# Counting two microseconds more, in the kernel's own scheduler, until a transfer of rotated heads has landed

## The chip, the cores and the metric

The kernel runs on one core of one Trainium2 chip. Five engines of that core matter here: TensorE (PE in the profile, with its weight loads as PEld), VectorE (DVE), ScalarE (ACT), GpSimd (POOL) and SyncE (SP), whose queue issues every DMA of this kernel. The metric is device time in microseconds; lower is better. "Before" is a median of three runs, and one further execution was taken by the hardware profiler, which gives the span (first to last instruction) and all rows quoted below.

## The reference

A decoder trunk with 256 tokens of width 1024 and two layers, all in float32. The first layer is causal multi-head latent attention (MLA), the second is MoBA block-sparse attention over keys and values computed once from the stream after the first layer. With 256 tokens there is a single MoBA block, so the second layer is in effect causal attention with 16 heads of 64. Each layer ends in a gated output projection, a residual and a LayerNorm.

```python
def moba_shared_kv(x, w_kv, cos, sin):
    kv = x @ w_kv
    k = kv[..., :WIDTH_B].reshape(B, S, H_B, HD_B)
    v = kv[..., WIDTH_B:].reshape(B, S, H_B, HD_B)
    k = apply_rope(k, ...)

def moba_mixer(x, k_blocks, v_blocks, k_mean, w_in, w_o, cos, sin):
    h = x @ w_in
    q, gate = h[..., :WIDTH_B], h[..., WIDTH_B:]
    q = apply_rope(q.reshape(B, S, H_B, HD_B), ...)
    ...                                   # scores, causal mask, softmax, values
    return (o * jax.nn.silu(gate)) @ w_o

def reference(x, ...):
    for layer in range(DEPTH):
        ...
        x = layer_norm(ALPHA * x + y, ln_g[layer], ln_b[layer])
    return x
```

## The kernel before, in words

**Arithmetic.** Every float32 weight and activation is split into a rounded part and a remainder (the tiles `wh` and `wl`, `act_h` and `act_l`, `big_h` and `big_l`; ACT casts, DVE or POOL subtracts). A product is then three matmuls: high by high, low by high, high by low. Two groups of products matter below. A *chunk* is a product of 128 output features by 256 tokens over 8 slices of the inner dimension, 24 matmuls of 256 columns into a PSUM bank called `proj`. A *token product* has 128 tokens as output partitions and 512 (or 258, or 256) features as columns.

**Stages.** First the MLA layer; its output projection (`oa`), LayerNorm, and the value projection of the second layer (`vb`). Then the stage that the change touches, the MoBA attention, from about 160 us on. It has 24 chunks: eight of queries (`qb`), eight of keys (`kb`), eight of gates (`gb`). Then the output projection (`ob`), whose result is kept for token half 0 in two `proj` banks and for token half 1 in two `s` banks and one `proj` bank, followed by the last LayerNorm.

**Rotated heads and their transfers.** `rope_moba` makes one chunk of queries and one of keys in a bank, multiplies by cosine and sine (DVE), adds halves (POOL or DVE) and splits the result into the tile `R` (named `x_h`). The heads' rows then have to change partitions: `move_heads` does this with eight DMAs for each pair of heads, four of 96 KB and four of 64 KB, from `R` into one of three tiles `HT` (`kq0`, `kq1`, `x_l`), so that rows `kq<-x_h` and `x_l<-x_h` in the profile are these transfers. The scores of a pair of heads (`s<-kq` or `s<-x_l`, three matmuls a head) need all eight. After the scores come, for each head: mask and exponent (tile `e`; DVE and ACT), three transposes on PE (`pt<-ident,e`), a copy by ACT, and for every two pairs the products with the values (`pv<-pt,V`), which DVE multiplies by the gates into `oa` and ACT, POOL and DVE split into `big_h` and `big_l`, the left operand of the output projection.

**What sets the order.** Nothing is issued in the order of the source. Every operation is recorded with an estimated duration, and `Schedule.order` replays the program on paper: for each engine it keeps what is ready, and puts down next the operation that can start first, with priorities from the longest way to the end and the place in the source. Each engine then executes its list strictly in the written order; waits are semaphores. A transfer ends on paper at its queue start, plus its size, plus 1300 ns, plus a constant that its caller may give:

```python
x = max(t + 1100, dma)
dma = x + o.size / 330.0
o.end = dma + 1300 + o.late
lanes.append(o.end + 100)
```

`late` is 2000 for seven of the eight first loads of inputs and weights (`LATE`) and zero for everything else. `lanes` holds the paper's ends of transfers; with `LANES` (8) of them open, the next transfer waits on paper.

**The end of the program.** `token_products("ob", ...)` goes over the eight slices of the inner dimension, token half 1 lagging by eight. Slices 6 and 7 of the weights lie in the tiles `x_h` and `x_l`, so rows `proj<-x_h,big_h` and `proj<-x_l,big_h` are the last slices of token half 0, and `s<-x_h,big_h` those of token half 1. When token half 0 is complete, `finish_b` runs `layer_norm` on DVE in pieces of 512 columns (residual, statistics, two passes with gain and bias; rows with tile `m`, `bst`, `mv`). `last_b` does the same for token half 1 in pieces (0 to 512, 512 to 768, 768 to 1024): rows `m<-m,s`, `bst<-m`, `ms`, `act_h<-m,ms,lng`, and last `act_h<-act_h,mv,lnb`, after each of which but the first a store to the output is issued.

Of the kernel before, what the change touches and what calls it, by code (L numbers as in the profile page):

```python
# [53 lines left out]
PLAIN = 2  # L54
PIECES = 4
LATE = 2000

LANES = 8

# [79 lines left out]
def A(x):  # L139
    if isinstance(x, View):  # L140
        return x.ap()
    return x.tile() if isinstance(x, Val) else x
# [225 lines left out]
def trunk(ctx, tc, W0, xtok, W, WO, gq, gkv, lng, lnb, cosa, sina, coska, sinka, cosb, sinb, maskd, identd, out):  # L368
# [22 lines left out]
    def dma(o, i, size, part=False, r=None, late=0):  # L391
        sc.op("sp", 650 if part else 525, lambda: nc.sync.dma_start(A(o), A(i)), [i] if r is None else r, [o], size).late = late
# [55 lines left out]
    def split(h, l, src, n, scale=None, eng="dve"):  # L448
        if scale is None:
            act(h, src, n)  # L450
            tt(l, src, h.f32(), ALU.subtract, n, eng)
        else:
            act(h, src, n, AF.Identity, scale=scale)
            stt(l, src, scale, h.f32(), ALU.mult, ALU.subtract, n)
# [10 lines left out]
    def load_raw():  # L465
# [3 lines left out]
        if u < 8:  # L469

            for c0, c1 in ((0, 512), (512, 1280)) if u < PLAIN else ((0, 1280),):
                dma(r[:, c0:c1].at(c0), W0[u, :, c0:c1], (c1 - c0) * 512, late=LATE * (u > 0))
            split(xh[:, u, :].at(u), xl[:, u, :].at(u), r[:, 0:S].at(0), S)
# [128 lines left out]
    for k in range(8):  # L602
        w = weights("g1", k)
        a, b = xs(k)
        for c in range(8):
            o = g1[c // 2][:, (c % 2) * S:(c % 2) * S + S]
            if k < PLAIN and c < 2:
                u, v = first_raws[k][:, S + c * P:S + (c + 1) * P].at(0), first_raws[k][:, 0:S].at(0)
# [323 lines left out]
    def move_heads(step):  # L932
        while moves and moves[0][0] - 3 <= step:
            p, R, base = moves.pop(0)
            hd = HT[p % 3]
            for s in range(2):
                r0 = base + 32 * s
                for v in range(2):
                    dma(hd[32 * v:32 * v + 32, s, 0:3, :].at((s, v, 0)).f32(), R[r0:r0 + 32, v, 1:4, :].at(None).f32(), 98304, True)
                    dma(hd[64 + 32 * v:96 + 32 * v, s, 0:2, :].at((s, v, 1)).f32(), R[r0:r0 + 32, v, 0:4:2, :].at(None).f32(), 65536, True)  # L940

    def heads_moba(p):
        hd = HT[p % 3]
# [6 lines left out]
    def fill_b(step):  # L950
        for nm, i in PLAN_B[step + 1]:
            if nm == "r":
                rope_moba(i)
            else:
                gate("gb", i, x1s)
            move_heads(step)
        move_heads(step)
# [153 lines left out]
```

## Time and profile before

| | |
|---|---|
| median of 3 runs | 276.71 us (275.78 to 276.76) |
| the profiled execution | 275.99 us |
| its span | 274.2 us |
| around the span | 1.8 us |
| PE busy, weight loads busy | 267.3 us (97%), 246.3 us (90%) |
| DVE busy | 217.0 us (79%) |
| ACT busy | 164.1 us (60%) |
| POOL busy | 44.8 us (16%) |
| DMA | 52.46 MB, mean 191 GB/s |
| transfers of rotated heads | 64 in all, median 2.1 to 2.5 us from issue to landing by tile and size |
| MoBA attention | from 159.84 us |
| output projection | first matmul at 242.31 us, last at 267.88 us |
| last DVE instruction | from 269.59 us, for 1.67 us with the three before it |

How to read it: a matmul's record holds its whole way through the array, so consecutive ones overlap and a busy PE says little; whether PE waited is seen from the distance between two starts. A row of the timeline gives start, duration, engine, line, operation, output and inputs, shapes and count; in square brackets stands idle time of the engine before it, with what ended it. The line numbers of rows are those of the kernel before; in the changed kernel all lines from the new constant on are two higher.

### The profile page before, as it was taken

How to read it: one execution, taken by the hardware profiler on the slowest of the kernel's cores; microseconds unless marked ns; L12 is line 12 of the kernel's file. 1: busy time of each engine (PE TensorE's matmuls, PEld its weight loads, DVE VectorE, ACT ScalarE, POOL GpSimd, SP SyncE). 2: the span in 40 equal slices, each digit the busy share in tenths (PEclk: the TensorE clock that was granted, in tenths of full speed). 3: DMA queues.
4: the chain of work that ended last, by engine and by line, in shares of the span. 5: the costliest groups of instructions: out<-in, count | busy, mean ns of one | idle time of the engine just before them, and what ended most of it. 6: DMA issues, size and time to landing. Idle time of an engine off the chain costs nothing.

```text
span 274.2 us, 5384 instructions
## 1 busy us (share of the span) xinstructions
PE 267.3 (97%) x1950; PEld 246.3 (90%) x1950; DVE 217.0 (79%) x494; ACT 164.1 (60%) x366; POOL 44.8 (16%) x46
## 2 busy tenths in 40 slices
PE   8999999999999999999999999999999999999991
PEld 6999999999899988878888899999999999887890
DVE  3776889999998789947997436879978998897584
ACT  4864977477774779914372543637856859986000
POOL 3000162300020021111010000602324214021000
PEclk9999999999999999999999999999999999999998
DMA  7999484777334442470459574466759768440022
GB/s 232 405 400 412 164 278 183 238 266 274 115 118 149 158 155 78 138 247 0 148 175 295 203 255 154 155 187 195 273 128 331 200 220 322 117 127 4 0 78 77
DMA packets 18683, 52.46 MB, mean 191 GB/s; under 512 B 2912, under 2 KB 6112, under 8 KB 18656
## 3 DMA queue, kind: packets, MB, share of 16 engines
q1 hardware_dynamic: 18656, 52.12, 56.4%
q8 instruction: 15, 0.25, 0.4%
q14 instruction: 12, 0.10, 0.1%
HBM read 45.81 MB, written 1.05 MB: 171 GB/s over the span
## 4 chain that ended last, share of the span: by engine, by line
PE 93%; issue 3%; DVE 2%; POOL 0%; POOLq 0%; DVEq 0%
PE proj L430 61%; PE s L430 15%; PE pv L430 8%; PE pt L444 5%; PE pt L430 4%; DVE bst L864 1%; DVE m L415 0%; DVE act_h L415 0%; POOL mv L411 0%; POOLq L1107 0%; DVEq L1107 0%; DVE mv L865 0%; DVE mv L422 0%
## 5 line engine op out<-in xcount | busy, mean ns | idle before, releaser
L411 DVE TENSOR_TENSOR wl<-raw,wh 128x1024 fp32r<-128x1024 f32 (+3 forms) x80 | 85.6, 1090 | 21.3 <-ACT wh L400 21.0
L400 ACT CAST wh<-raw 128x1024 fp32r<-128x1024 f32 (+4 forms) x81 | 73.5, 925 | 36.6 <-PE proj L430 17.8
L430 PE MATMUL proj<-act_h,wh 128*128 128x256 f32 x280 | 79.6, 284 | 0.0
L430 PE MATMUL proj<-act_l,wh 128*128 128x256 f32 x280 | 78.5, 280 | 0.0
L430 PE MATMUL proj<-act_h,wl 128*128 128x256 f32 x280 | 78.5, 280 | 0.0
L430 PEld LDWEIGHTS proj<-act_h,wh 128*128 128x128 f32 x280 | 52.8, 188 | 0.0
L430 PEld LDWEIGHTS proj<-act_l,wh 128*128 128x128 f32 x280 | 52.7, 188 | 0.0
L430 PEld LDWEIGHTS proj<-act_h,wl 128*128 128x128 f32 x280 | 52.7, 188 | 0.0
L404 ACT ACTIVATE e<-e,st 128x256 f32<-128x256 f32 x64 | 28.5, 449 | 6.3 <-DVE st L770 6.2
L411 POOL TENSOR_TENSOR big_l<-oa,big_h 128x256 fp32r<-128x256 f32 x14 | 10.8, 786 | 87.7 <-ACT big_h L400 87.7
L430 PE MATMUL s<-kq 128*128 128x256 f32 (+1 forms) x100 | 19.1, 318 | 0.0
L424 DVE TENSOR_SCALAR e<-e,st 128x256 f32<-128x256 f32 x64 | 18.0, 325 | 0.9
L430 PE MATMUL proj<-x_h,wh 128*128 128x256 f32 x64 | 18.5, 289 | 0.0
L430 PE MATMUL proj<-x_h,wl 128*128 128x256 f32 x64 | 18.0, 281 | 0.0
L430 PE MATMUL proj<-x_l,wh 128*128 128x256 f32 x64 | 18.0, 281 | 0.0
L430 PEld LDWEIGHTS s<-kq 128*128 128x128 f32 x100 | 15.6, 190 | 1.6 <-issue 0.3
L400 ACT COPY pt<-pt 128x384 f32<-128x384 f32 x32 | 14.8, 477 | 1.5 <-PE pt L444 1.3
L411 DVE TENSOR_TENSOR x_l<-raw,x_h 128x256 fp32r<-128x256 f32 (+2 forms) x14 | 10.7, 770 | 5.9 <-ACT x_h L400 5.9
L444 PE MATMUL pt<-ident,e 128*128 128x128 f32 x96 | 15.0, 275 | 0.1
L400 ACT CAST x_h<-raw 128x256 fp32r<-128x256 f32 (+2 forms) x14 | 9.4, 685 | 8.7 <-PE s L430 4.3
L411 POOL TENSOR_TENSOR t<-t,t512b 128x512 f32<-128x512 f32 x5 | 6.8, 1364 | 39.0 <-DVE t L411 21.4
L444 PEld LDWEIGHTS pt<-ident,e 128*128 128x128 f32 x96 | 11.0, 140 | 1.4 <-issue 0.7
(190 smaller groups left out, 570.6 us busy)
## 6 DMA issues: line engine op xcount, KB each, us to landing
raw<-in_W SPq DMA_DIRECT2D x58, 512.0 KB, 4.4
raw<-in_WO SPq DMA_DIRECT2D x8, 528.0 KB, 5.4
raw<-in_W SPq DMA_DIRECT2D x6, 640.0 KB, 6.9
raw<-in_W SPq DMA_DIRECT2D x6, 384.0 KB, 5.9
kq<-x_h SPq DMA_DIRECT2D x24, 96.0 KB, 2.2
kq<-x_h SPq DMA_DIRECT2D x24, 64.0 KB, 2.1
m<-in_xtok SPq DMA_DIRECT2D x2, 512.0 KB, 6.4
lng<-in_lng SPq DMA_DIRECT2D x2, 512.0 KB, 3.6
```

The lines of the kernel that those rows point to most:

```text
L400: nc.scalar.copy(A(o), A(i))
L404: nc.scalar.activation(A(o), A(i), func, bias=A(bias), scale=A(scale), accum_out=A(accum))
L411: sc.op(eng, dur, lambda: e.tensor_tensor(A(o), A(a), A(b), op=op), [a, b], [o], lock=not (is_ps(a) or is_ps(b)))
L424: fn = lambda: e.tensor_scalar(A(o), A(a), A(s1), s2, op0=op0, op1=op1)
L430: nc.tensor.matmul(A(out_), A(lt), A(rh), start=st, stop=sp_, skip_group_check=True)
L444: nc.tensor.transpose(A(x), A(y), A(ident))
L864: sc.op("dve", 600, lambda hf=hf, cs=cs: nc.vector.bn_stats(A(st[:, hf, :]), A(z[:, cs])), [z.at(hf)], [st.at(hf)])
```

## The change

A constant `MOVE_LATE` of 2000 is added, and the two `dma` calls in `move_heads` pass it as `late`. No instruction is added, removed or given another operand: the counts of matmuls, DVE instructions and transfers are equal. Only the order in which they stand on each engine differs, from the scores of the first MoBA heads on.

```diff
--- before.py
+++ after.py
@@ -54,6 +54,8 @@
 PLAIN = 2
 PIECES = 4
 LATE = 2000
+
+MOVE_LATE = 2000
 
 LANES = 8
 
@@ -936,8 +938,8 @@
             for s in range(2):
                 r0 = base + 32 * s
                 for v in range(2):
-                    dma(hd[...], R[r0:r0 + 32, v, 1:4, :].at(None).f32(), 98304, True)
-                    dma(hd[...], R[r0:r0 + 32, v, 0:4:2, :].at(None).f32(), 65536, True)
+                    dma(hd[...], R[r0:r0 + 32, v, 1:4, :].at(None).f32(), 98304, True, late=MOVE_LATE)
+                    dma(hd[...], R[r0:r0 + 32, v, 0:4:2, :].at(None).f32(), 65536, True, late=MOVE_LATE)
```

Three places of the new order matter below.

**DVE at the first MoBA scores.** Before (`wl<-raw,wh` is the remainder of a weight slice, `e<-s,masks` the first step of a head's softmax):

```order
L411 TENSOR_TENSOR t512b<-proj,sinbs 128x512
L411 TENSOR_TENSOR t_2257<-t_2257,t512b 128x512
L411 TENSOR_TENSOR e<-s,masks 128x128
L770 ISA e,st<-s,masks 128x256
L770 ISA st 128x1
```

And now:

```order
L413 TENSOR_TENSOR t512b<-proj,sinbs 128x512
L413 TENSOR_TENSOR t_2257<-t_2257,t512b 128x512
L413 TENSOR_TENSOR wl<-raw,wh 128x1024
L413 TENSOR_TENSOR e<-s,masks 128x128
L772 ISA e,st<-s,masks 128x256
```

One more weight slice is split ahead of the first head's softmax, for 18 more chunk matmuls stand on PE ahead of the first scores.

**PE at the last slices of token half 0** (`proj<-x_h,big_h` and its two companions, twelve matmuls in all). Before, they follow the first group of token half 1:

```order
L430 MATMUL s<-wh,big_h 128x512
L430 MATMUL s<-wl,big_h 128x512
L430 MATMUL s<-wh,big_l 128x512
L430 MATMUL proj<-x_h,big_h 128x512
L430 MATMUL proj<-x_l,big_h 128x512
L430 MATMUL proj<-x_h,big_l 128x512
```

And now they follow the third group of 258 columns:

```order
L432 MATMUL s<-wh,big_h 128x258
L432 MATMUL s<-wl,big_h 128x258
L432 MATMUL s<-wh,big_l 128x258
L432 MATMUL proj<-x_h,big_h 128x512
L432 MATMUL proj<-x_l,big_h 128x512
L432 MATMUL proj<-x_h,big_l 128x512
```

Of token half 1, five more groups of three matmuls of 512 columns and three groups of three of 258 columns now stand in front of them. The last products with the values, which feed slices 6 and 7, have moved back too: two groups of 512 and three of 258 columns lie between them and the first `proj<-x_h,big_h`, where three `proj` groups and one `s` group, all of 512 columns, were (a `proj` or `s` group is three matmuls).

**DVE in the last LayerNorm** (`m_293` is token half 0, `m_320` token half 1, `lng` gain, `lnb` bias). Before:

```order
L415 SCALAR_TENSOR_TENSOR m_293<-m_293,mv,lng 128x512 x2
L415 SCALAR_TENSOR_TENSOR m_293<-m_293,mv,lnb 128x512 x2
L415 SCALAR_TENSOR_TENSOR m_320<-m_320,s 128x512
L996 BN_STATS bst_3380<-m_320 128x6 x2
L422 TENSOR_SCALAR bst_3380<-bst_3380 128x1
L415 SCALAR_TENSOR_TENSOR m_320<-m_320,s 128x256
L415 SCALAR_TENSOR_TENSOR ms<-s,ms 128x1
```

And now:

```order
L417 SCALAR_TENSOR_TENSOR m_293<-m_293,mv,lng 128x512
L417 SCALAR_TENSOR_TENSOR m_320<-m_320,s 128x512
L417 SCALAR_TENSOR_TENSOR ms<-s,ms 128x1
L998 BN_STATS bst_3391<-m_320 128x6
L417 SCALAR_TENSOR_TENSOR m_293<-m_293,mv,lng 128x512
L417 SCALAR_TENSOR_TENSOR m_293<-m_293,mv,lnb 128x512 x2
L998 BN_STATS bst_3391<-m_320 128x6
L424 TENSOR_SCALAR bst_3391<-bst_3391 128x1
L417 SCALAR_TENSOR_TENSOR m_320<-m_320,s 128x256
```

The instructions are the same; the first ones of token half 1 now stand among those of token half 0.

More of the change, by code (lines that the diff above doesn't have):

```diff
@@ L938, in move_heads @@
                 for v in range(2):
-                    dma(hd[32 * v:32 * v + 32, s, 0:3, :].at((s, v, 0)).f32(), R[r0:r0 + 32, v, 1:4, :].at(None).f32(), 98304, True)
-                    dma(hd[64 + 32 * v:96 + 32 * v, s, 0:2, :].at((s, v, 1)).f32(), R[r0:r0 + 32, v, 0:4:2, :].at(None).f32(), 65536, True)
+                    dma(hd[32 * v:32 * v + 32, s, 0:3, :].at((s, v, 0)).f32(), R[r0:r0 + 32, v, 1:4, :].at(None).f32(), 98304, True, late=MOVE_LATE)
+                    dma(hd[64 + 32 * v:96 + 32 * v, s, 0:2, :].at((s, v, 1)).f32(), R[r0:r0 + 32, v, 0:4:2, :].at(None).f32(), 65536, True, late=MOVE_LATE)
     def heads_moba(p):
```

## The prediction, made blind

> **What bounds the kernel now.** I read the page first (busy shares and the chain that ended last), then the distances between starts on TensorE in the stage that the change reorders, then the end of the program on every engine. The page:
>
> ```profile
> span 274.2 us, 5384 instructions
> PE 267.3 (97%) x1950; PEld 246.3 (90%) x1950; DVE 217.0 (79%) x494; ACT 164.1 (60%) x366; POOL 44.8 (16%) x46
> PE 93%; issue 3%; DVE 2%; POOL 0%; POOLq 0%; DVEq 0%
> ```
>
> 93% of the chain is PE: the kernel is a long train of matmuls, with a short tail on other engines. So two questions decide: is there any wait on PE that the new order could remove, and does the tail stay as it is?
>
> For the first, the timeline of PE where the first scores of MoBA stand, and what the view of the tile `kq` says of its transfers (minimum, median and maximum from issue to landing; who waited):
>
> ```profile
> 186.22 0.28 PE L430 MATMUL proj<-act_h,wl 128*128 128x256 f32 x1
> 186.34 0.88 PE L430 MATMUL s<-kq 128*128 128x256 f32 x6
>   issue: 0.2, 1
>   ACT x_h L400: 1.5, 1
> DMA to landing us min/median/max: 2.0/2.1/5.8
> 177.81 10.52 SPq L392 DMA_DIRECT2D kq<-x_h  x16
> ```
>
> The scores start 0.12 us after the matmul in front of them: they did not wait. Their eight transfers are the first half of sixteen issues from 177.81 us on, so the last was issued near 183.1 and, at the median, landed near 185.2, 1.1 us early. The only instruction that the view shows waiting for these transfers is one on ACT, 1.5 us, off the chain.
>
> What all waits of PE in the stage can be worth comes from the table by stretches, for PE; the first two rows are the `proj` matmuls alone, the last two are all matmuls (time, busy, count):
>
> ```profile
> 159.84:186.34 26.50, 26.50 (x225) 1.00 0.56 180
> 186.34:242.31 55.97, 44.43 (x353) 1.00 0.71 222
> ...
> 159.84:186.34 26.50, 26.50 (x227) 1.00 0.56 180
> 186.34:242.31 55.97, 55.97 (x485) 1.00 0.71 222
> ```
>
> and from the chain of waits the price of a head's transposes and of two pairs' value products:
>
> ```profile
> 245.25 0.33 PE pt L444 x3
> 250.07 1.45 PE pv L430 x16
> ```
>
> In the first stretch 225 `proj` matmuls take 26.50 us, 0.1178 us each, without a score or transpose among them. Of the second's counts two are overlaps at the edge: 351 `proj` matmuls (576 of 24 chunks less 225), and 132 others, which are 45 of scores, 39 transposes and 48 of values. At those prices (396 x 0.1178 + 13 x 0.33 + 3 x 1.45) they need 55.3 of the 55.97 us. So all waits and changes of operand kind in the MoBA attention are **at most 0.7 us**. That is the ceiling of what any order of these chunks can win.
>
> **The change part by part.** It adds and removes no instruction; every price is one of position.
>
> *The scores move back.* 18 chunk matmuls (2.1 us) now stand ahead of the first scores. Nothing waited for the transfers, so nothing is won there; a gain from fewer waits elsewhere in the stage lies between 0 and 0.7 us, a loss from softmax chains that have less time before their transposes between 0 and some tenths. I take 0 for the stage: the new order puts 30 matmuls (3.5 us) between the first scores and the first transposes where 27 were, so these chains are not squeezed. On SP one more weight load now stands ahead of the transfers of the third pair:
>
> ```profile
> 188.43 2.88 SPq L392 DMA_DIRECT2D raw<-in_W  x4
> 193.16 4.82 SPq L392 DMA_DIRECT2D x_l<-x_h  x7
> ```
>
> An issue costs 0.72 us (2.88 / 4), and SP stood idle for 1.85 us between the two blocks (191.31 to 193.16), so the fifth load fits in. It needs a free weight buffer first, and behind it on SP are these transfers; the split that frees a buffer has moved ahead on DVE as well (ahead of the first softmax). I cost it at 0, and if it blocks, at the 0.72 us.
>
> *The end of token half 0 moves back.* This is the term that counts. The timeline of PE at the end, one row where each kind of group begins, and the last row:
>
> ```profile
> 254.34 0.40 PE L430 MATMUL proj<-x_h,big_h 128*128 128x512 f32 x1
> ...
> 257.14 0.39 PE L430 MATMUL s<-wh,big_h 128*128 128x512 f32 x1
> ...
> 260.61 0.39 PE L430 MATMUL s<-x_h,big_h 128*128 128x512 f32 x1
> ...
> 262.00 0.28 PE L430 MATMUL s<-wh,big_h 128*128 128x258 f32 x1
> ...
> 264.91 0.40 PE L430 MATMUL proj<-act_l 128*128 128x256 f32 x2
> ...
> 267.88 0.27 PE L430 MATMUL proj<-x_h,big_l 128*128 128x256 f32 x1
> ```
>
> Prices: the twelve `proj<-x` 2.80 us; fifteen `s` of 512 columns 3.47; six `s<-x` 1.39; 24 of 258 columns 2.91, so 0.121 each; the last 26 to 268.00 (one step of 0.12 behind the last start) 3.09. Before, 13.66 us of PE work lay between the first `proj<-x_h` and the end. Now fifteen of 512 and nine of 258 columns have gone ahead of it: 3.47 + 1.09 = 4.56 us less lie behind, 9.10 us. PE's work as a whole is unchanged, so PE ends where it did, 268.00, and the first `proj<-x_h` starts at 258.90. The LayerNorm of token half 0 therefore starts **4.56 us later**. What DVE then has to do stands in its timeline (rows between these are small statistics):
>
> ```profile
> 256.63 0.69 DVE L415 SCALAR_TENSOR_TENSOR m<-m,proj 128x512 f32<-128x512 f32 x1 [3.04 <-PE proj L430]
> ...
> 259.71 1.41 DVE L415 SCALAR_TENSOR_TENSOR m<-m,mv,lng 128x512 f32<-128x512 f32 x2
> 261.03 1.41 DVE L415 SCALAR_TENSOR_TENSOR m<-m,mv,lnb 128x512 f32<-128x512 f32 x2
> 262.36 0.68 DVE L415 SCALAR_TENSOR_TENSOR m<-m,s 128x512 f32<-128x512 f32 x1
> 263.07 0.75 DVE L996 BATCH_NORM_STATS2 bst<-m 128x6 f32<-128x256 f32 x2
> ...
> 265.11 0.42 DVE L415 SCALAR_TENSOR_TENSOR m<-m,s 128x256 f32<-128x256 f32 x1 [1.23 <-PE s L430]
> ...
> 268.19 0.43 DVE L996 BATCH_NORM_STATS2 bst<-proj 128x6 f32<-128x256 f32 x1 [0.42 <-PE proj L430]
> ...
> 269.59 1.67 DVE L415 SCALAR_TENSOR_TENSOR act_h<-act_h,mv,lnb 128x256 f32<-128x256 f32 x4 [0.34 <-POOL mv L411]
> 270.50 1.30 SPq L392 DMA_DIRECT2D out<-act_h  x3
> ```
>
> From 256.63 to 271.26 (269.59 + 1.67) DVE has 14.63 us in which it waited for PE twice, 1.23 and 0.42 us, and once for POOL. Before, PE sets the pace of the tail and DVE has that 1.65 us to spare. A start 4.56 us later uses it up, and the rest comes out at the end: 4.56 - 1.65 = **2.91 us**.
>
> I check that DVE indeed never waits for PE in the new tail, with the order as it now stands. First residual at 258.90 + (256.63 - 254.34) = 261.19; the first pass with the gain 3.08 later, 264.27; 0.66 on, at 264.93, the first residual of token half 1, whose bank was done near 258.90 + 2.80 + 1.39 = 263.1; 0.71 on, at 265.64, the row `ms`, whose bank is done near 265.1. The last bank is done at 268.2, and DVE comes to it 3.07 us (271.26 - 268.19) before its end, 274.17 - 3.07 = 271.1. So from 261.19 on DVE works without a break and ends at 261.19 + 14.63 - 1.65 = 274.17. The stores follow as before: the span ended 274.2 - 271.26 = 2.94 us behind DVE's last instruction. The wait for POOL (0.34) stays, since the same statistics precede it.
>
> *The last value products move back.* Before the first `proj<-x_h` there is now one group less between the value products and their use. The rows that carry this:
>
> ```profile
> 251.45 0.50 PE L430 MATMUL proj<-wh,big_h 128*128 128x512 f32 x1
> 248.72 2.43 DVE L411 TENSOR_TENSOR x_l<-raw,x_h 128x1056 fp32r<-128x1056 f32 x2 [1.00 <-ACT x_h L400]
> 252.87 0.72 DVE L411 TENSOR_TENSOR big_l<-oa,big_h 128x256 fp32r<-128x256 f32 x1 [0.47 <-ACT big_h L400]
> ```
>
> The values end where the next group starts, 251.45; the last remainder is ready at 253.59, 2.14 us later, and was used 2.89 us or more later (254.34). Now two groups of 512 columns (0.8 and 0.69 us) and nine matmuls of 258 (1.09) lie between: 2.58 us to the first use of slice 6 and 1.4 more to that of slice 7. The cover is thinner by 0.3 us and holds; I cost it at 0. If the cover is gone, because one of the two `x_l` splits (2.43 us for two) stands in front of DVE's gate products, it costs up to 1.2 us.
>
> Sum against the profiled execution: 275.99 + 2.91 + 0 + 0 = 278.9 us. That execution lies 0.72 us under the median of the three runs and 0.21 over their lowest; from the median it would be 279.6. I take **279.2 us**, 0.9% slower.
>
> [...]
>
> **The rivals.**
>
> *No change, about 276.7 us.* PE's work is the same, PE is 97% busy and 93% of the chain, so the time is the same. It decides if DVE can absorb the 4.56 us, for which it needs that much idle time behind 256.63; the rows show 1.65 for PE. Chance 0.08. [...]
>
> *Faster, about 276.0 us.* The order gives transfers and softmax chains more room, PE loses the 0.7 us of waits and changes, and the tail does not grow. For it speaks only that a transfer once took 5.8 us; against it that no matmul waited for one. The gain alone is 0.7 us; with the tail as worked out, 278.5. Chance of the first 0.03.
>
> *Slower still, about 280.4 us.* PE stands for up to 1.2 us in front of the last slices or the last transposes, since ACT and DVE now have the last weight casts and splits among the softmax of the last heads. That moves PE's end and the tail behind it together: 279.2 + 1.2. Against it: 0.4 us of margin by the rows above. Chance 0.13.
>
> That the change does nothing is out: the order of PE, DVE, ACT and SP differs from the first scores on.
>
> **How the numbers follow.** The likeliest, DVE as the tail's bound, has 0.76: 279.2, with its own range 278.0 (0.7 us won on PE, from the lowest of the three runs) to 280.0. The range that should hold the time 8 times in 10 reaches to the slower case: **277.8 to 280.7 us**; left out are the first two rivals. What a measurement of this kernel can tell from no change is about 0.5%, 1.4 us. Slower by more than that: 0.76 + 0.13 less 0.02 for the edge of the likeliest, 0.87. Within it: 0.08 and that edge, 0.10. Faster by more: 0.03.
>
> **What would show it.** In the changed profile: the first `proj<-x_h,big_h` at 258.9 and PE's last start near 267.9; the LayerNorm of token half 0 from 261.2; no idle time of DVE for PE between there and the end; DVE's last instruction ending near 274.2 and a span near 277.1; a chain whose last 13 us are DVE. I am wrong if DVE still shows waits for PE in the tail, if PE ends earlier by more than 0.7 us, or if the transposes or slices 6 and 7 wait.

## The result and the profile after

The changed kernel takes **279.71 us**, a median of six executions (279.40 to 280.18), against 276.08 us for six of the kernel before (275.33 to 276.76) beside it. The ratio on record is 1.0121, with a 95% interval of 1.0097 to 1.0145 (the quotient of the two medians, 1.0131, lies inside it): slower by 1.2%. The profiled execution took 279.67 us with a span of 277.9 us, 3.7 us more than before. Two executions of the kernel before among the experiments' runs (279.85 and 279.98 us) were in a slower state and enter no comparison.

The page of the changed kernel, to be held against the three rows that open the prediction (busy time and count of each engine, then the shares of the chain that ended last):

```profile
PE 266.8 (96%) x1950; PEld 245.7 (88%) x1950; DVE 219.9 (79%) x494; ACT 164.6 (59%) x366; POOL 45.2 (16%) x46
PE 89%; DVE 6%; issue 3%; ACT 0%; POOL 0%; POOLq 0%; DVEq 0%
```

The counts are the same and PE's busy time is even 0.5 us shorter. What changed is the chain: DVE's share went from 2% to 6%, and DVE itself is busy 2.9 us longer with the same 494 instructions. So DVE stands at the end of the program now, and some of its instructions have become longer. The two are different stories, and the trace shows both.

The first: the end of the program, PE's rows.

```profile
259.85 0.39 PE L432 MATMUL proj<-x_h,big_h 128*128 128x512 f32 x1
...
268.85 0.28 PE L432 MATMUL proj<-x_h,big_l 128*128 128x256 f32 x1
```

And DVE's rows of the same stretch:

```profile
258.68 0.73 DVE L413 TENSOR_TENSOR big_l<-oa,big_h 128x256 fp32r<-128x256 f32 x1 [0.47 <-ACT big_h L402]
262.14 0.69 DVE L417 SCALAR_TENSOR_TENSOR m<-m,proj 128x512 f32<-128x512 f32 x1 [2.73 <-PE proj L432]
...
265.88 0.68 DVE L417 SCALAR_TENSOR_TENSOR m<-m,s 128x512 f32<-128x512 f32 x1
266.48 0.15 DVE L417 SCALAR_TENSOR_TENSOR ms<-s,ms 128x1 f32<-128x1 f32 x1
...
273.27 1.67 DVE L417 SCALAR_TENSOR_TENSOR act_h<-act_h,mv,lnb 128x256 f32<-128x256 f32 x4 [0.34 <-POOL mv L413]
```

PE ends at 268.97 (one step of 0.12 us behind its last start), 0.97 us later than before. From the first `proj<-x_h,big_h` to PE's end there are 9.12 us instead of 13.66. DVE runs from 262.14 to 274.94 without a wait for PE and ends 5.97 us behind PE, where it was 3.26. So of DVE's 3.68 us (274.94 against 271.26), **2.71 us are the tail** and **0.97 us came from PE**, both in these two executions.

The second story is PE's 0.97 us. They are a difference of two things that have to be kept apart. The last matmul ahead of the MoBA attention, in the kernel before and in the changed kernel:

```profile
159.60 0.40 PE L430 MATMUL pv<-x_h,act_l 128*128 128x512 f32 x1
159.06 0.40 PE L432 MATMUL pv<-x_h,act_l 128*128 128x512 f32 x1
```

The profiled execution of the changed kernel came into the stage 0.54 us earlier. Up to there every engine executes the same instructions in the same order in both kernels, so this is no effect of the change: over all fourteen profiles of this document the same matmul starts anywhere from 158.63 to 159.80 us. From that start to PE's end it is 108.40 us before and 109.91 now. So **within the stage PE lost 1.51 us**, and 0.54 us of chance hide a part of it. The loss is the largest distance between two starts of matmuls in the attention stage. PE's rows of the changed kernel there:

```profile
193.07 0.28 PE L432 MATMUL proj<-act_h,wl 128*128 128x256 f32 x1
194.84 0.55 PE L446 MATMUL pt<-ident,e 128*128 128x128 f32 x3 [1.49 <-DVE e L426]
```

1.77 us lie between the starts, 0.12 would do (consecutive matmuls of 256 columns start 0.12 us apart, with records of 0.28 us): PE stood 1.65 us for the scaled exponents of the second head of the first pair (the rest of the stage is 0.14 us shorter). What DVE and POOL did there, each in its timeline (first DVE, then POOL):

```profile
190.92 0.55 DVE L426 TENSOR_SCALAR e<-e,st 128x256 f32<-128x256 f32 x2
191.39 0.68 DVE L413 TENSOR_TENSOR t512b<-proj,sinbs 128x512 f32<-128x512 f32 x1
...
192.18 2.61 DVE L426 TENSOR_SCALAR e<-e,st 128x256 f32<-128x256 f32 x2
194.71 1.21 DVE L413 TENSOR_TENSOR wl<-raw,wh 128x1024 fp32r<-128x1024 f32 x1
```

```profile
186.44 1.60 POOL L413 TENSOR_TENSOR t<-t,t512b 128x512 f32<-128x512 f32 x1 [8.43 <-DVE t512b L413]
192.15 2.55 POOL L413 TENSOR_TENSOR x_h<-t,x_h 128x512 fp32r<-128x512 f32 x2 [4.11 <-DVE st L778]
```

The same pair of scaling passes takes 0.55 us at 190.92 and 2.61 us at 192.18. It did not wait at its head for anything; it was long. It began 0.03 us behind POOL's two remainders, which take 2.55 us, and ended 0.09 us behind them (194.79 against 194.70). One by one, the first pass took 1.41 us and ended 0.15 us behind POOL's first remainder, and the second took 1.28 us and ended 0.08 us behind POOL's second. In the kernel before, the same work of POOL lay between two pairs of scaling passes: that of the second head had ended 0.26 us ahead of it (191.58), and the next began 0.15 us behind it (194.40):

```profile
191.84 2.56 POOL L411 TENSOR_TENSOR x_h<-t,x_h 128x512 fp32r<-128x512 f32 x2 [3.24 <-DMA raw<-in_W]
```

```profile
191.03 0.55 DVE L424 TENSOR_SCALAR e<-e,st 128x256 f32<-128x256 f32 x2
194.55 0.54 DVE L424 TENSOR_SCALAR e<-e,st 128x256 f32<-128x256 f32 x2
```

So the theories to be tested are: (T) the place of token half 0's last slices against 12.8 us of DVE work sets the tail; (S) the length of DVE's scaling passes beside POOL's remainders (2.61 us against 0.55) sets PE's loss in the stage. The rivals: that later scores cost by themselves, evenly with the number in the constant; that PE's end and not DVE's work set the tail; and that a third cause hides in the new order.

### The profile page after: what moved, and what is told of

It reads as the page before. It is cut to its first block, busy times and chain, and to the rows that moved or that the text cites. A ratio compares the mean times of both kernels' runs of the same rounds, so it can differ in the third digit from the quotient of the medians.

```text
span 277.9 us, 5383 instructions
## 1 busy us (share of the span) xinstructions
PE 266.8 (96%) x1950; PEld 245.7 (88%) x1950; DVE 219.9 (79%) x494; ACT 164.6 (59%) x366; POOL 45.2 (16%) x46
## 4 chain that ended last, share of the span: by engine, by line
PE 89%; DVE 6%; issue 3%; ACT 0%; POOL 0%; POOLq 0%; DVEq 0%
PE proj L432 57%; PE s L432 16%; PE pv L432 7%; PE pt L446 5%; PE pt L432 4%; DVE e L426 1%; DVE wl L413 1%; DVE bst L866 1%; DVE t L413 0%; DVE m L417 0%; DVE e L772 0%; DVE act_h L417 0%; ACT e L406 0%; POOL mv L413 0%; DVE t512b L413 0%
## 5 line engine op out<-in xcount | busy, mean ns | idle before, releaser
L413 DVE TENSOR_TENSOR wl<-raw,wh 128x1024 fp32r<-128x1024 f32 (+3 forms) x80 | 87.0, 1108 | 22.3 <-ACT wh L402 22.0
L426 DVE TENSOR_SCALAR e<-e,st 128x256 f32<-128x256 f32 x64 | 20.1, 357 | 0.9
L413 POOL TENSOR_TENSOR t<-t,t512b 128x512 f32<-128x512 f32 x5 | 7.7, 1552 | 39.0 <-DVE t L413 20.9
```

Of the source, the lines that this page charges most:

```text
L413: sc.op(eng, dur, lambda: e.tensor_tensor(A(o), A(a), A(b), op=op), [a, b], [o], lock=not (is_ps(a) or is_ps(b)))
L426: fn = lambda: e.tensor_scalar(A(o), A(a), A(s1), s2, op0=op0, op1=op1)
```

## The experiments

In all tables "behind" is the time from the first `proj<-x_h,big_h` to PE's end, and the tail is DVE's end less PE's end. The kernels below were timed in four series, each with its own executions of the kernel before. Their medians were 276.5 us (for the first three sections), 277.0 (POOL's work, the tail's order put back, the constant of 2500), 276.3 (three groups put back, 500 and 1000) and 277.2 us (1500). Times of different series are therefore compared by their ratios, each of which stands with its interval, and where tenths matter the positions in the profiles decide; there "the stage" is the time from the last matmul ahead of the MoBA attention to PE's end.

Single executions of the kernel before spread over 3.3 to 4.0 us within a series, and so do those of other kernels that keep the old order of the scores or nearly so: over 2.4 us in twelve executions of the one without four DVE passes, over 3.1 us in twelve with 500 in the constant. Those with 1000 or more spread over 0.8 to 1.6 us. One reason shows in the profiles of two kernels with the old order of PE there (the tail's order alone, and the kernel before without four DVE passes). They came into the stage 0.46 and 0.29 us earlier than the profiled execution of the kernel before, and then a matmul of scores waited for its transfer of rotated heads, for which the profile of the kernel before shows no wait:

```profile
238.29 0.59 PE L438 MATMUL s<-kq 128*128 128x256 f32 x3 [0.51 <-DMA kq<-x_h]
```

```profile
238.34 0.62 PE L430 MATMUL s<-kq 128*128 128x256 f32 x3
```

(First the tail's order alone, then the kernel before.) The stage took 108.79 and 108.76 us in these two, against 108.40. With 500 in the constant such a wait of 0.36 us stands at 217.36; in none of the ten profiles with 1000 or more does a matmul wait for one. So the change does take away a wait that the one profile of the kernel before does not show, worth about 0.4 us where it was seen. That it accounts for the whole spread is not shown.

### The tail's order alone, in the kernel before

All transfers count as before; only the eight groups of token half 1 are put ahead of slice 6 of token half 0, as the change does.

```diff
-                    dma(..., True, late=MOVE_LATE)
+                    dma(..., True)
...
         self.out = self.order()
+        ahead = [o for o in self.out if o.tag in [(1, j) for j in (1, 2, 3, 4, 5, 8, 9, 10)]]
+        self.out = [o for o in self.out if o not in ahead]
+        at = [o.tag for o in self.out].index((0, 6))
+        self.out[at:at] = ahead
```

> The kernel before, with one part of the new order alone: on TensorE five groups of 512 columns and three of 258 of token half 1 stand ahead of the last two slices of token half 0, as in the changed kernel; every other engine's order is that of the kernel before. Theory (DVE bounds the tail): the LayerNorm of token half 0 starts 4.56 us later against an unchanged end of PE, DVE uses up 1.65 us of waits, so the time grows by 2.7 to 2.9 us, to 278.9 from 276.1, with no stall of PE near 190 us. Rival (the tail costs nothing and the whole 3.6 us comes from the stall of the transposes and what it pushes): 276.1, no change.

Measured: 279.87 us (278.66 to 281.19, six executions), ratio 1.0101 (1.0064 to 1.0139). PE's and DVE's last rows in its profile (an execution of 278.66 us):

```profile
267.81 0.28 PE L438 MATMUL proj<-x_h,big_l 128*128 128x256 f32 x1
```

```profile
272.23 1.67 DVE L423 SCALAR_TENSOR_TENSOR act_h<-act_h,mv,lnb 128x256 f32<-128x256 f32 x4 [0.34 <-POOL mv L419]
```

PE ends at 267.93, close to the kernel before (268.00; it came into the stage 0.46 us earlier and lost 0.51 us to the wait shown above), and DVE 5.97 us behind it. The tail's share, 2.7 us, comes from this order and needs nothing of the rest of the change.

### DVE's work taken out of the tail, in both kernels

The four passes with gain and bias over token half 0 in the last LayerNorm do nothing; the order of all else is kept.

```diff
-    def layer_norm(banks, res, z, gb, bb):
+    def layer_norm(banks, res, z, gb, bb, final=False):
...
+            if final:
+                sc.ops[-1].fn = lambda: None
```

In the changed kernel:

> The changed kernel in its own order, but the four DVE passes with gain and bias over token half 0 in the last LayerNorm (2.64 us of DVE) are left out, so that half of the output is not normalised. Theory (DVE bounds the tail from the first residual on): the time falls by 2.6 us, all that is left out, to 277.1; what then remains over the kernel before is the 1 us by which PE ended later. Rival (the tail is paced by PE, as before the change): DVE only waits more, the time stays at 279.7.

In the kernel before:

> The kernel before in its own order with the same four DVE passes left out. Theory (before the change PE paces the tail, and DVE had 1.65 us of waits there): DVE waits 2.64 us longer for PE and the time stays at 276.1. Rival (DVE bounded the tail before as well): 273.5.

Measured: the changed kernel goes to 277.25 us, ratio 1.0015 (0.9995 to 1.0035) in place of 1.0121; by the profiles its span falls from 277.9 to 275.4 us. The kernel before stays: 276.55 us, ratio 0.9996 (0.9970 to 1.0022). Why it stays shows in DVE's waits there:

```profile
262.26 0.69 DVE L415 SCALAR_TENSOR_TENSOR m<-m,s 128x512 f32<-128x512 f32 x1 [2.40 <-PE s L430]
265.18 0.42 DVE L415 SCALAR_TENSOR_TENSOR m<-m,s 128x256 f32<-128x256 f32 x1 [1.39 <-PE s L430]
268.26 0.43 DVE L1000 BATCH_NORM_STATS2 bst<-proj 128x6 f32<-128x256 f32 x1 [0.42 <-PE proj L430]
```

What the passes took (2.82 us, two rows of 1.41) became waiting for PE: 4.21 us in place of 1.65. In the changed kernel the same removal leaves one wait for PE of 0.15 us in the tail, and the end moves. Before, PE paced the tail; after the change, DVE does.

### One sine product moved on DVE

In the changed kernel the product `t512b<-proj,sinbs` of chunk 4, which stood between the scaling passes of the first and the second head, comes behind the second's.

```diff
         self.out = self.order()
+        x = [o for o in self.out if o.tag == ("sin", SIN)][0]
+        y = [o for o in self.out if o.tag == ("nm", "b", 0, 1, 1)][0]
+        self.out.remove(x)
+        self.out.insert(self.out.index(y) + 1, x)
```

> The changed kernel with two neighbours on DVE exchanged near 191.4 us: the second head's normalising of the exponents (2.61 us in the changed profile beside two POOL instructions, 0.55 elsewhere) comes ahead of the product with the sines. Theory (POOL's two instructions with two SBUF inputs hold up that DVE instruction, and its transposes then hold up PE by 1.65 us): it is done before POOL starts, takes 0.55 us, PE's gap of 1.77 us near 193 goes, and the time falls by 1.0 to 1.6 us, to 278.1 to 278.7; DVE still bounds the tail. Rival (the normalising is slow for another reason, or the gap is made up later): the gap or the time stays, 279.7.

Measured: 278.25 us (277.87 to 278.85, twelve executions), ratio 1.0052 (1.0031 to 1.0074) in place of 1.0121; the span falls from 277.9 to 276.3 us. DVE's scaling passes and weight split, then POOL:

```profile
191.76 0.55 DVE L436 TENSOR_SCALAR e<-e,st 128x256 f32<-128x256 f32 x2
192.82 1.72 DVE L423 TENSOR_TENSOR wl<-raw,wh 128x1024 fp32r<-128x1024 f32 x1
```

```profile
192.11 3.58 POOL L423 TENSOR_TENSOR x_h<-t,x_h 128x512 fp32r<-128x512 f32 x2 [4.11 <-ACT x_h L412]
```

The pair takes 0.55 us again, PE's gap is gone, and PE ends at 267.40. DVE and POOL still meet: now the weight split takes 1.72 us instead of 1.21, and POOL's two remainders 3.58 instead of 2.55. No matmul waits for either. PE ends 1.57 us earlier than in the changed kernel, and the stage is 1.53 us shorter (108.38): that is the price of the stall. Without it the stage is as long as in the profile of the kernel before (108.40). That PE ends 0.60 us earlier than there is no gain of the new order, since this execution came into the stage 0.58 us earlier (159.02).

### POOL's work taken from that place

In the changed kernel, with no instruction moved, POOL's remainders of the second group of rotated heads become copies. The expectation speaks of four; the profile shows that there are two, those of the stall.

```diff
             split(R[:, v, 1:3, :].at((v, 0)), R[:, v, 0:4:3, :].at((v, 1)), t, 512, eng=on("rl", g, v))
+            if g == 1:
+                sc.ops[-1].fn = lambda v=v, t=t: nc.gpsimd.tensor_copy(A(R[:, v, 0:4:3, :].at((v, 1))), A(t))
```

> The changed kernel, its order unchanged on every engine, but the four remainders of group 1's rotated heads on POOL are a copy of the first operand (one input in SBUF) in place of a difference of two; the low part of these heads is left out of the result. Theory (DVE's scaling pass stands while POOL works on two inputs in SBUF): the pair of scaling passes near 192 us takes 0.55 again, the transposes no longer stand 1.5 us, PE ends 1.0 to 1.6 us earlier than 268.97, the time is 278.1 to 278.7 us, ratio 1.007 to 1.009. Rival (any work of POOL holds it up, one input as well): the pair takes until POOL's copies end; if a copy takes as long as the difference, 2.6 us and no gain, 279.7; if it takes half, some 1.3 us and half the gain. Rival (the pair was late for another reason, a semaphore among them): 2.6 us still, with POOL long done.

Measured: 278.13 us (277.66 to 278.46), ratio 1.0040 (1.0014 to 1.0067). POOL, then DVE:

```profile
190.06 1.17 POOL L933 CAST x_h<-t 128x512 fp32r<-128x512 f32 x2 [1.61 <-DMA kq<-x_h]
```

```profile
187.23 2.31 DVE L413 TENSOR_TENSOR wl<-raw,wh 128x1024 fp32r<-128x1024 f32 x1
191.34 0.55 DVE L426 TENSOR_SCALAR e<-e,st 128x256 f32<-128x256 f32 x2
192.59 0.55 DVE L426 TENSOR_SCALAR e<-e,st 128x256 f32<-128x256 f32 x2
```

The pair takes 0.55 us with DVE's order unchanged. PE ends 1.26 us earlier than in the changed kernel (267.71) although it came into the stage 0.42 us later (159.48), so the stage is 1.68 us shorter (108.23). That is the size expected of the first theory, and it shows that DVE's own order without POOL's work beside it makes no stall. It does not tell one input from two: a copy need not wait for ACT's high part, so the copies ran 2.1 us earlier and were over before either pair began. The weight split at 187.23 kept its 2.31 us beside a sum on POOL (186.86, 1.60 us) that was left as it was.

### The tail's order put back, alone and together with the sine product

In the changed kernel the eight groups go back behind slices 6 and 7 of token half 0; in the second kernel the sine product is moved as well.

```diff
+        ahead = [o for o in self.out if o.tag in [(1, j) for j in (1, 2, 3, 4, 5, 8, 9, 10)]]
+        self.out = [o for o in self.out if o not in ahead]
+        for js, j in (((1, 2, 3, 4, 5), 6), ((8, 9, 10), 11)):
+            at = [o.tag for o in self.out].index((1, j))
+            self.out[at:at] = [o for o in ahead if o.tag[1] in js]
```

The first:

> The changed kernel in which only the last projection's order on PE is put back: the five 512-wide and three 258-wide groups of token half 1 that now stand ahead of the slices 6 and 7 of token half 0 stand behind them again, as in the kernel before. All else, the stand of the DVE beside POOL near 192 us among it, is as in the changed kernel. Theory (two causes, which add): the tail's share goes, the stall's stays. PE's last product ends at 268.97 as in the changed kernel, DVE ends 3.26 us behind it as in the kernel before, so the execution is 2.71 us shorter than the changed one: 277.0 us, ratio to before 1.003 to 1.005. Rival (later scores cost by themselves, wherever the slices stand): still above 279. Rival (the tail alone was all of it, the stall is caught up elsewhere): 276.0 to 276.3.

Both:

> Both at once: the slices of token half 0 back in front as in the kernel before, and on DVE the sine product of rope chunk 4 behind the normalising of the second head. The transfers of rotated heads count 2000 more still. Theory: PE's last product ends at 267.40 as it did with the second of these alone, DVE 3.26 us behind it at 270.7, which is 0.6 us earlier than in the kernel before: 275.4 to 275.7 us in the execution, ratio 0.998. Rival (a third cause in the changed order): ratio 1.003 or more, with DVE or PE standing somewhere else than in the two places.

Measured: 281.27 us, ratio 1.0168 (1.0128 to 1.0209), and 280.11 us, ratio 1.0122 (1.0085 to 1.0159). Both expectations failed. The first kernel is slower than the changed one by its profile (span 279.6 against 277.9 us; the intervals of the ratios overlap), and the second is clearly slower than with the sine product alone (1.0122 against 1.0052). PE's rows of the first at the end of the attention:

```profile
253.33 0.52 PE L455 MATMUL pt<-ident,e 128*128 128x128 f32 x3
253.78 2.22 PE L441 MATMUL pv<-pt,V 128*64 128x256 f32 x16
257.02 0.50 PE L441 MATMUL proj<-x_h,big_h 128*128 128x512 f32 x1 [1.02 <-ACT big_h L411]
...
271.01 0.27 PE L441 MATMUL proj<-x_h,big_l 128*128 128x256 f32 x1
```

and of the changed kernel:

```profile
254.00 0.49 PE L446 MATMUL pt<-ident,e 128*128 128x128 f32 x3
...
255.81 1.52 PE L432 MATMUL pv<-pt,V 128*64 128x256 f32 x16
```

With the groups away, PE stands inside the value products (2.22 us instead of 1.52) and for 1.02 us behind them, until the last heads' `big_h` is there, and ends at 271.13, 2.16 us later. In the changed kernel eight groups lay from just ahead of the last transposes to the first `proj<-x_h,big_h`: they cover the last heads' way from PE over ACT and DVE back to PE. I had overlooked that. The last values are 5.7 us later than before (255.81 against 250.07 in the chain that the prediction shows), and the groups of token half 1 are what is left to fill in.

The tail did not go back to 3.26 us either. It is 5.51 (DVE ends at 274.97 + 1.67 = 276.64), by this row:

```profile
268.24 0.16 DVE L426 SCALAR_TENSOR_TENSOR ms<-s,ms 128x1 f32<-128x1 f32 x1 [2.23 <-PE s L441]
```

This row now waits for token half 1's second bank, and the three remaining passes over token half 0 are queued behind it. In the order before they stand ahead of token half 1; the change moved them on DVE, and I put back PE's order alone. So these two runs were no clean undoing, and a kernel with DVE's order put back too was not run. From the first one's rows it would end at some 271.13 + 3.26 = 274.4, against 274.94 in the changed kernel: an estimate, not shown by a run, by which the price of the later heads is paid in nearly the same amount on either engine, by DVE's work behind PE's end (2.71 us) or by PE's standing (2.16 us).

### Three of the eight groups put back

With the sine product moved, of the eight groups only one of 512 and two of 258 columns go back.

```diff
+        keep = [o for o in self.out if o.tag in [(1, 3), (1, 4), (1, 5), (1, 9), (1, 10)]]
+        self.out = [o for o in self.out if o not in keep]
+        for before, js in (((1, 8), (3, 4)), ((1, 6), (5,)), ((1, 11), (9, 10))):
+            at = [o.tag for o in self.out].index(before)
+            self.out[at:at] = [o for o in keep if o.tag[1] in js]
```

> The order of the run that moved one sine product on DVE, and beside it three groups of token half 1 (one 512-wide, two 258-wide, 0.69 + 2 * 0.37 = 1.43 us of PE) put back behind token half 0's slices 6 and 7: of the two 512-wide groups between the last transposes and the last value products one stays, and behind the value products 1.75 us of the 2.59 us stay. With all eight groups put back PE stood 1.02 us before the first product of the last slices and began that product 1.83 us before it had its last operand, so that 1.75 us should just cover it. Theory (the tail is a balance: what stands ahead of the last slices costs DVE's tail its whole length, what is taken away beyond the cover costs PE's standing): the first product of the last slices comes 1.4 us earlier, PE stands at most 0.4 us more, the time is 278.25 - 1.43 = 276.8 to 277.2 us, ratio 1.000 to 1.003. Rival (any group taken away there is paid by PE's standing, in full): 278.2 us, ratio 1.005, with new idle time of PE of 1.4 us between 252 and 258 us.

Measured: 277.53 us (277.19 to 278.42), ratio 1.0063 (1.0040 to 1.0085). The expectation of 1.000 to 1.003 failed: by the ratios nothing is won over the sine product alone (1.0052, 1.0031 to 1.0074). By the profiles DVE ends 0.5 us earlier (272.87 against 273.38), a third of the 1.43 us expected. PE did as the theory says: its first `proj<-x_h,big_h` is at 256.83, 1.46 us earlier than with the sine product alone (258.29), it stands nowhere, and it ends at 267.35. The rest went here, on DVE:

```profile
264.46 0.16 DVE L432 SCALAR_TENSOR_TENSOR ms<-s,ms 128x1 f32<-128x1 f32 x1 [0.92 <-PE s L447]
```

The two groups of 258 columns that went back belong to the bank whose last column this row reads. They make that bank 0.92 us too late for DVE, and the tail shrinks from 5.97 to 5.52 us only (DVE's end, 271.20 + 1.67, less 267.35). It is the same DVE order as in the two runs above: token half 0's passes wait behind this row. The rival is out, for PE has no new idle time; the theory lacked DVE's order.

### Other numbers in the constant

The changed kernel with 500, 1000, 1500 and 2500 in place of 2000, each in the order that comes out.

```diff
-MOVE_LATE = 2000
+MOVE_LATE = 1000
```

500:

> The changed kernel with 500 in place of 2000. In the order that comes out one group of token half 1 stands ahead of the last slices, as in the kernel before, so the tail is that of the kernel before. Theory: ratio 0.998 to 1.002, unless DVE's passes meet POOL's work in SBUF in the attention stage, which would show as a pass of twice its length and PE idle by as much. Rival (the number's size as such): a quarter of 3.6 us, 277.0, ratio 1.003.

1000:

> The changed kernel with 1000 in place of 2000. In the order that comes out five 512-wide groups of token half 1 stand ahead of the last slices of token half 0 and no 258-wide one: the work behind the first product of these slices is 10.88 us, against 13.66 us in the kernel before and 9.10 us with 2000. Theory (the place of these slices sets the tail): DVE ends 2.29 + 12.98 - 10.88 - 3.26 = 1.13 us later, 277.0 to 277.6 us with no stall beside it, ratio 1.003 to 1.005. Rival (the number's size as such): half of the change's 3.6 us, 277.9.

1500:

> The changed kernel with 1500 in place of 2000. In the order that comes out one 512-wide group of token half 1 fewer than with 1000 stands ahead of the last slices: work behind their first product 11.58 us, so DVE's tail grows by 2.29 + 12.98 - 11.58 - 3.26 = 0.43 us, and PE ended 0.66 us earlier than in the kernel before with 1000. Theory (place of the slices, whatever the number, and the scores' wait that really goes): 275.6 to 276.3 us, ratio 0.997 to 1.000, less than with 1000; if DVE's passes meet POOL's work near 192 us it is up to 1.7 us more, seen there. Rival (the number's size as such, three quarters of the change's 3.6 us): 278.8 us, ratio 1.010.

2500:

> The changed kernel with 2500 in place of 2000. By the order that comes out, all groups of width 512 and 258 of token half 1 and 15 products of the next width stand ahead of token half 0's last slices: the work behind the first product of slice 6's last part is 5.98 us. Theory (place of these slices against DVE's work of 12.98 us behind them): DVE ends 2.29 + 12.98 - 5.98 - 3.26 = 6.0 us later than PE's end would ask, 282.0 to 283.0 us with no stall elsewhere, and up to 1.7 us more if DVE and POOL meet again. Rival (the later scores themselves cost, evenly with the number): 276.1 + 3.6 * 1.25 = 280.6.

What was measured, with the positions from the profiles:

| constant | time, us | ratio (95% interval) | behind | tail | PE's end | stage | stall near 193 |
|---|---|---|---|---|---|---|---|
| 0 (before) | 276.08 | 1 | 13.66 | 3.26 | 268.00 | 108.40 | none |
| 500 | 275.91 | 0.9988 (0.9959 to 1.0016) | 13.66 | 3.26 | 268.15 | 109.52 | none |
| 1000 | 276.30 | 1.0007 (0.9988 to 1.0026) | 10.88 | 4.20 | 267.34 | 108.24 | none |
| 1500 | 277.31 | 1.0001 (0.9977 to 1.0024) | 11.58 | 3.51 | 269.30 | 110.00 | 1.65 us |
| 2000 (the change) | 279.71 | 1.0121 (1.0097 to 1.0145) | 9.12 | 5.97 | 268.97 | 109.91 | 1.65 us |
| 2500 | 281.25 | 1.0166 (1.0128 to 1.0203) | 6.00 | 9.09 | 267.33 | 108.30 | none |

Each ratio is to the kernel before of the same series, so the times of different rows do not compare directly.

The tail follows the column "behind" and not the constant: in the four rows in which DVE has no wait for PE in it, "behind" and tail add up to 15.08 or 15.09 us, which is DVE's 12.80 us of work and the 2.29 from the first `proj<-x_h,big_h` to the first residual. 1500 has a shorter tail than 1000, since one group fewer stands ahead. From 1000 on the stage goes by the stall: 108.2 to 108.3 us without it and 109.9 to 110.0 with it. (With 500 two other waits of PE, 0.36 us for a transfer and 0.37 for ACT, make it longer.) 1500 shows the stall in the same rows as the change, its pair of scaling passes and POOL's remainders:

```profile
192.43 2.61 DVE L426 TENSOR_SCALAR e<-e,st 128x256 f32<-128x256 f32 x2
```

```profile
192.40 2.55 POOL L413 TENSOR_TENSOR x_h<-t,x_h 128x512 fp32r<-128x512 f32 x2 [4.11 <-DVE st L778]
```

With 1000 POOL's remainders stand at the same time (192.40, 2.55 us), but DVE's pair is already done:

```profile
191.49 0.55 DVE L426 TENSOR_SCALAR e<-e,st 128x256 f32<-128x256 f32 x2
```

The expectations for 500 and, with the stall that it names, 1500 were met in time, though 1500's ratio of 1.0001 is not what its profile alone would give: the kernel before took 277.2 us in that series, and 275.99 in its profile. That for 1000 was 0.7 us too high and that for 2500 0.75 us. In both profiled executions PE ended 0.66 and 0.67 us earlier than in that of the kernel before, and 0.50 and 0.57 us of this were there when PE came into the stage. With 2500 the time speaks for the rival: its 280.6 us, 1.6% above the 276.1 that both start from, lies inside the interval of the ratio, and the theory's 282.0, 2.1% above, does not. What decides is the tail of 9.09 us, 5.83 longer where 6.0 was expected, and 1000 and 1500, at which the rival's 277.9 and 278.8 us (ratios of 1.007 and 1.010) were not reached. In the end none of these numbers beats the kernel before by what can be measured.

## Why the prediction was right, and where it was not

The forecast was 279.2 us in a range of 277.8 to 280.7; 279.71 was measured. The main case held. Against the profiled execution the sum gave 278.9, and 279.67 was measured: 0.8 us short, of which the 0.3 us added for the other executions' sake hid a part. The tail was 0.20 us too large in it and PE's end 0.97 us too early. That the miss is no larger is in part luck: the loss in the stage, put at 0, was 1.51 us, and the profiled execution happened to come into the stage 0.54 us early. Step by step:

- **"The end of token half 0 moves back", 2.91 us.** Right: 2.71 us. The 9.10 us of work behind the first `proj<-x_h,big_h` were 9.12, and DVE had no wait for PE from there on. The 0.20 us too much is a mis-sized term: DVE's work was put at 14.63 - 1.65 = 12.98 us and took 12.80.
- **"PE's work as a whole is unchanged, so PE ends where it did".** This failed by 0.97 us, and by 1.51 us within the stage. The step behind it is "I take 0 for the stage", with a loss of at most "some tenths" because "these chains are not squeezed". The count of 30 matmuls for 27 is right, but it ends at the first head's transposes. PE waited at the second head's, and up to these there are 39 matmuls for 42. By an estimate from the rows the squeeze alone would have been harmless: of its usual length the pair would have ended at 192.73, and PE came to these transposes near 193.19. What cost the time is that the pair became 2.06 us longer (2.61 against 0.55), which no count of matmuls shows. Undoing it by moving one sine product made the stage 1.53 us shorter.
- **A gain "between 0 and 0.7 us" on PE, left at 0.** Against the profile of the kernel before the stage without a stall is 0.02 to 0.17 us shorter (108.38 to 108.23), so 0 was right for that execution. The premise that nothing waited for the transfers held for that execution; two others, with the same order on PE up to there, waited 0.51 us for one.
- **The extra weight load on SP, 0.** No wait of PE in the changed kernel answers to it; the one large gap was DVE's.
- **"The last value products move back", 0.** Right, with less margin than the rows ahead of it suggest. The last remainder ended at 259.41 (258.68 + 0.73) and the first `proj<-x_h,big_h` began at 259.85. What the step did not see is that the groups which delay DVE's tail are the same that cover these products: with them put back PE ended 2.16 us later.
- **The rivals.** "No change" needed 4.56 us of spare time on DVE. Without four passes the kernel before did not get faster and the changed one did, so the spare time was used up. "Slower still" named PE's standing at the last slices or last transposes; PE did stand, but at the first heads, 60 us ahead, so this rival was right that PE would stand and wrong in its place.
- **The signs named beforehand.** The first `proj<-x_h,big_h` came at 259.85 for 258.9, the LayerNorm at 262.14 for 261.2, DVE's end at 274.94 for 274.2, all 0.7 to 1.0 us late, by PE's 0.97 less, at the end, the tail's 0.20. Of the signs of being wrong one did show, "if the transposes wait": those of the second head did, by 1.49 us.

PE's share, from which "No change" was argued, went from 97% to 96% and that of the weight loads from 90% to 88%, while the loads' busy time stayed (246.3 and 245.7 us) and the time grew by 3.6 us: the share shows that the span grew around equal work, not where. The 2.71 us lie behind PE's end.

## What to carry to other kernels

An order that leaves the busiest engine's work unchanged can still move the end: look for the last piece of work that another engine must do behind it, sum that engine's rows from its earliest start, and compare with what is left on the busy engine. Before calling such an order a slip, ask what the moved work was covering; here taking it back on PE alone cost 2.16 us there, and DVE's order, made for the other one, gave back only 0.46 us of the tail. And when an order changes, look at which DVE passes now run beside POOL's, since here a pair of passes became almost five times as long (2.61 us against 0.55) with no wait in front of it. Last, compare two executions from the place where their orders part: here half a microsecond of the difference in PE's end was there before.

## What the hardware showed that I had not expected

Some of DVE's and POOL's passes became longer where they ran beside each other, by most of what was left of the other's instructions. The pair of scaling passes (0.55 us alone) took 2.61 us, 2.06 more, where 2.52 us of POOL's 2.55 were left as it began, and ended 0.09 us behind them; it was the same with 1500 in the constant (2.61 beside 2.55). A weight split, 1.22 us in the median, took 2.31 us when it began beside a POOL sum:

```profile
186.81 2.31 DVE L413 TENSOR_TENSOR wl<-raw,wh 128x1024 fp32r<-128x1024 f32 x1
```

That POOL sum ran from 186.44 to 188.04, so 1.23 us of it were left; the split became 1.09 us longer and ended 1.08 us behind it. The other way round, with the sine product moved, POOL's two remainders took 3.58 us (192.11 to 195.69) in place of 2.55 where a weight split (192.82 to 194.54) fell among them: they ended 1.15 us behind the split. In the kernel before the same remainders (191.84 to 194.40, 2.56 us) lay beside mask passes, which read the scores from PSUM (0.41 and 0.42 us, 0.41 in the mean of all such), and beside a reciprocal of two columns (0.16 us, as in the mean), and neither side became longer:

```profile
191.70 0.41 DVE L770 CUSTOM_DVE_ANT_0 e<-s,masks 128x256 f32<-128x256 f32 x1
192.45 0.42 DVE L770 CUSTOM_DVE_ANT_0 e<-s,masks 128x256 f32<-128x256 f32 x1
193.89 0.16 DVE L776 RECIPROCAL st<-st 128x2 f32<-128x2 f32 x1
```

What the two engines contend for is not shown by any run here, nor is what sets the passes that became longer apart from those that did not; shown are the lengths, 2.61 us beside 2.55 in the stall and 0.55 without. Whether a POOL pass with a single input has this effect as well is not shown here either, since the copies that were to show it ran too early.
